# Weight sums of a seven-product block multiplication formed by accumulating transfers, with another order and other signs of the products

## The chip, the cores and the metric

The kernel runs on one core of a Trainium2 chip. Its engines are TensorE (PE, matmuls; PEld is its weight loader), VectorE (DVE), ScalarE (ACT), GpSimd (POOL) and SyncE (SP). Transfers (DMA) are issued from the queues of SP, ACT and POOL. The metric is the device time of one execution in microseconds (us). Of the kernel before, three runs were timed: median 1592.65 us, 1592.23 to 1593.92.

## The reference

One hybrid layer: normalised tokens `xn` (256 tokens, 2048 channels) and 256 context tokens `cn` are multiplied with slices of one large weight `w_in`; two branches (window attention, and a gated recurrence over 16 heads) follow, then a merge and an output projection. What matters here are two kinds of these products:

```python
aq, ak, av, ag, hq, hff, hfb, hi, hg, ma, mb = split_columns(xn @ w_in[l])
caq, cak, cav, cag, chq, chff, chfb, chi, chg, cma, cmb = split_columns(cn @ w_in[l])
g_f, k_f = hgrn_forget(hff, lb_f_all[l])
g_b, k_b = hgrn_forget(hfb, lb_b_all[l])
cg_f, ck_f = hgrn_forget(chff, lb_f_all[l])
cg_b, ck_b = hgrn_forget(chfb, lb_b_all[l])
v_h = to_heads(hi)
cv_h = to_heads(chi)
```

A forget gate is `lb + (1 - lb) * sigmoid(z)`, of which the logarithm and the rest to one are used. Keys, values (`ak`, `av`, `hi`) and the forget gates (`hff`, `hfb`) are needed of all 512 tokens.

## The kernel before, in words

Every number of the activations and of the weights is kept as a sum of two parts, high and low, and a product is high by high, low by high and high by low. ACT makes the high part of a weight chunk (`wh`, 128x1024, 512 KB), DVE the low part (`wl` = weights less `wh`); there are three buffers of each.

The stage concerned runs from about 199 us to about 660 us. It computes the columns above as 2x2 block products with seven multiplications in place of eight (a scheme of Strassen's kind). The activations' four sums are formed once (`token_sums`, L570, tile `S`). For each weight block (four quarters 11, 12, 21, 22 of 512 KB) come a set of seven products, from seven weight operands: three plain quarters and four sums of quarters. There are 23 such sets:

- `quad_tok` (L687): ten sets, from 199 to 401 us. Five outputs, each two sets long; each of the seven products has a PSUM bank of its own. A product is 24 matmuls with 256 columns.
- `quad_col` (L639): thirteen sets, from 401 to 660 us, for the forget gates. The seven products share three banks. A product is eight matmuls with 512 columns (L660) and eight with 256 (L663).

The program orders TensorE's work as it is written; the other engines' orders come from a scheduler, in which `high_priority` puts marked steps ahead. `ORDER` (L608) gives the sequence of the products within a set, and `combos` (L611) yields the weight operands in that sequence. In the kernel before, the quarters are loaded by SP (`wload`, L61, five `raw` buffers), and DVE forms the four sums by four subtractions L616 (`t` = 12-11, then 22-`t`, 12-22 in its own buffer, 21-`t`); the tile `T` for `t` alternates between two buffers; `two` (L631) then makes high and low part (ACT L635, DVE L636).

In `quad_col` a product is added onto what stands in its bank, and at fixed points a bank's content is copied or added out while the sum goes on:

```python
into = {0: (0, True), 1: (1, True), 2: (0, False), 3: (1, False), 4: (0, False), 5: (2, True), 6: (0, False)}
```

The first entry is the bank, `True` starts it afresh. After products 0 and 1 ACT copies the bank to `s15` (L667); after product 2 ACT copies bank 0 to `su` (L670); after products 3, 4 and 5 DVE adds the bank to one of these copies (`joined`, L650, its adds are L653 and L654); after product 6 ACT and DVE take half a bank each (L678, L679). The gates then go through ACT (L682, L683) and out (L685). In the order 0, 1, 2, 3, 4, 5, 6 of the kernel before, the products go to banks 0, 1, 0, 1, 0, 2, 0.

Of the kernel before, what the change touches and what calls it, by code (L numbers as in the profile page):

```python
# [38 lines left out]
def block_kernel(ctx: ExitStack, tc: tile.TileContext, x, c, cx, c_ctx, w_ada, b_ada, norm_gain, w_in,  # L39
# [521 lines left out]
    with pl("sp", reuse_waits="tile") as sp:  # L561
# [8 lines left out]
        def token_sums(g):  # L570
# [7 lines left out]

            def put(i, t):
                ks = slice(4 * g, 4 * g + 4)  # L580
                dst = [S[:, z, i, ks, :].rearrange("p k t -> p (k t)") for z in range(2)]
                act.activation(dst[0], t, AF.Copy)
                dve.tensor_tensor(dst[1], t, dst[0].bitcast(F32), op=ALU.subtract)

# [4 lines left out]
            p, q = tmp(), tmp()  # L589
            step(v(p), a21[0], a22[0], ALU.add)  # L590
            step(v(q), a21[1], a22[1], ALU.add)
            step(p, p, q, ALU.add)
            put(0, p)
            step(v(q), v(p), a11[0], ALU.subtract)
            step(v(q), v(q), a11[1], ALU.subtract)
            put(1, q)
            for i, b in ((3, a12), (2, a22)):
                step(v(p), b[0], v(q), ALU.subtract)
                step(v(p), v(p), b[1], ALU.add)
                put(i, p)  # L600
# [10 lines left out]
        def combos(b):  # L611


            def sub(o, x_, y_):
                with tc.high_priority(PRIO):
                    dve.tensor_tensor(o, x_, y_, op=ALU.subtract)  # L616
# [12 lines left out]
            yield t  # L629

# [8 lines left out]
        def quad_col(d, h0):  # L639

            co = (C_FF, C_FB)[d] + h0 * HD
            b = {n: wload(w_in, 1024 * (n[0] == "2"), 8, (co + HD * (n[1] == "2"),), HD)[0]
                 for n in ("11", "12", "22", "21")}
            m_ = [bank8() for _ in range(3)]
# [10 lines left out]

            for (i, _, mv), src in zip(ORDER, combos(b)):
                h, lo = [a.rearrange("p (k c) -> p k c", k=8) for a in two(src)]
                z, fresh = into[i]
# [6 lines left out]
                with tc.high_priority(2 * PRIO):  # L665
                    if i < 2:
                        act.activation(s15[:, i, :], m_[i], AF.Copy)  # L667
                    elif i == 2:
                        su = base.tile([P, 512], F32, tag="bb", name="su", bufs=2)
                        act.activation(su, m_[0], AF.Copy)  # L670
                    elif i == 3:
                        joined(m_[1], su, half(sg[1], 0))
                    elif i == 4:
                        joined(m_[0], s15[:, 1, :], half(sg[1], 1))
                    elif i == 5:
                        joined(m_[2], s15[:, 0, :], half(sg[0], 0))
                    else:
                        act.activation(half(sg[0], 1), pairs_of(m_[0][:, T:]), AF.Copy)  # L678
                        dve.tensor_tensor(half(sg[0], 1), pairs_of(m_[0][:, :T]), half(sg[0], 1), op=ALU.add)  # L679
            F = fp.tile([P, 2, 512], F32, tag="F0", name="F0", bufs=2)  # L680
            for i in (1, 0):
                act.activation(sg[i], sg[i], AF.Sigmoid)  # L682
                act.activation(F[:, i, :], sg[i], AF.Identity, scale=lbc[:, 2 + d, h0 + i: h0 + i + 1],  # L683
# [3 lines left out]
        def quad_tok(col0, dst):  # L687
# [5 lines left out]
            def add(o, x_, y_):  # L693
                dve.tensor_tensor(o, x_, y_, op=ALU.add)

            def done_with(i):

# [4 lines left out]
                with tc.high_priority(2 * PRIO):  # L702
                    if i < 2:
                        sn[i] = base.tile([P, 512], F32, tag="sm", name="sn", bufs=3)
                        act.activation(sn[i], m_[i], AF.Copy)
                    elif i == 2:
                        sn[2] = base.tile([P, 512], F32, tag="bb", name="sn", bufs=2)
                        add(sn[2], m_[2], sn[0])
                    elif i == 3:
                        sn[3] = base.tile([P, 512], F32, tag="bb", name="sn", bufs=2)  # L710
                        add(sn[3], sn[2], sn[1])
                        add(place(0, 1), pairs_of(m_[3]), pairs_of(sn[3]))
                    elif i == 4:
                        add(sn[2], m_[4], sn[2])
                        add(place(1, 1), pairs_of(sn[2]), pairs_of(sn[1]))
                    elif i == 5:
# [4 lines left out]
            for s in range(2):  # L721
                b = {n: wload(w_in, 1024 * (n[0] == "2") + 512 * s, 4, (col0 + T * (n[1] == "2"),), T)[0]
                     for n in ("11", "12", "22", "21")}
                for (i, _, st_), src in zip(ORDER, combos(b)):
                    h, lo = [a.rearrange("p (k c) -> p k c", k=4) for a in two(src)]
                    if s == 0:
# [838 lines left out]
```

## Time and profile before

| what | value |
|---|---|
| three timed runs | 1592.65 us median, 1592.23 to 1593.92 |
| the profiled execution's own time | 1593.52 us |
| its span, first to last instruction | 1591.7 us |
| mean granted TensorE clock | 0.998 |
| TensorE busy | 1567.9 us, 99% of the span |
| VectorE busy | 1182.9 us, 74% |
| ScalarE busy | 855.4 us, 54% |
| GpSimd busy | 140.5 us, 9% |
| `w_in` loads of 512 KB from SP | 300, median 4.5 us to landing |

How to read the profile: in the timeline each row has the start, the duration, the engine, the line, the operation, its output and inputs, how many instructions were merged, and in brackets the engine's idle time ahead and what ended it. Names are without buffer numbers, so `s` is `s15`, `pj` and `pm` are PSUM banks, `raw` is any weight buffer. Matmuls overlap, so that the durations of neighbouring rows add up to more than the time between them; the distance of two starts is the safe measure. A busy PE is not a PE at its peak.

### The profile page before, as it was taken

What the parts mean: (1) busy time and instruction counts of PE and PEld (TensorE: products, weight loads), DVE (VectorE), ACT (ScalarE), POOL (GpSimd) and SP (SyncE); (2) the same over time, 40 slices, a digit from 0 to 9 for tenths busy, and PEclk for the clock granted to TensorE, in tenths of its full rate; (3) what the DMA queues carried; (4) which work ended last, traced back from release to release, by engine and by line L of the source; (5) the groups of instructions that cost most, each with busy time, mean ns of one, the idle gap of its engine ahead of it and who ended that gap; (6) DMA issues with size and microseconds to landing.
All of it is one profiled execution on the core that took longest, in us unless ns stands there. A gap on an engine that the chain in (4) does not pass through costs nothing. (4 is left out here: it accounts for less than half of the span.)

```text
span 1591.7 us, 27553 instructions
## 1 busy us (share of the span) xinstructions
PE 1567.9 (99%) x10810; PEld 1341.4 (84%) x10810; DVE 1182.9 (74%) x1745; ACT 855.4 (54%) x1338; POOL 140.5 (9%) x280
## 2 busy tenths in 40 slices
PE   7999999999999999999999999999999999999998
PEld 4567899999888888888888888888887888888887
DVE  4449677777888887787978888887976677757764
ACT  4334443333555555655665566666565776744442
POOL 2000000000000000111121212121112000000000
PEclk9999999999999999999999999999999999999999
DMA  9995533434444444777778777787778854458761
GB/s 369 386 387 174 166 110 131 134 131 133 146 133 136 136 135 130 243 234 230 245 264 271 256 259 244 238 271 240 234 262 262 261 165 149 158 175 288 238 196 70
DMA packets 240851, 333.81 MB, mean 210 GB/s; under 512 B 12080, under 2 KB 157904, under 8 KB 239952
## 3 DMA queue, kind: packets, MB, share of 16 engines
q1 hardware_dynamic: 212048, 249.54, 48.1%
q0 software_dynamic: 19168, 64.08, 11.9%
q10 hardware_dynamic: 9504, 18.42, 3.2%
q8 instruction: 85, 1.39, 0.4%
q14 instruction: 46, 0.38, 0.1%
HBM read 300.53 MB, written 31.47 MB: 209 GB/s over the span
## 5 line engine op out<-in xcount | busy, mean ns | idle before, releaser
L85 ACT ACTIVATE wh<-raw 128x1024 fp32r<-128x1024 f32 x292 | 307.5, 1060 | 257.3 <-PE pj L101 179.1
L86 DVE TENSOR_TENSOR wl<-raw,wh 128x1024 fp32r<-128x1024 f32 x292 | 354.4, 1219 | 122.1 <-ACT wh L85 116.2
L100 PE MATMUL pj<-wh,xHL 128*128 128x512 f32 (+1 forms) x832 | 325.0, 392 | 0.7 <-ACT sg L219 0.7
L101 PE MATMUL pj<-wh,xHL 128*128 128x512 f32 (+1 forms) x832 | 320.3, 386 | 0.0
L103 PE MATMUL pj<-wl,xHL 128*128 128x512 f32 (+1 forms) x832 | 218.5, 386 | 0.0
L100 PEld LDWEIGHTS pj<-wh,xHL 128*128 128x128 f32 x832 | 156.9, 189 | 32.7 <-ACT sg L219 1.9
L101 PEld LDWEIGHTS pj<-wh,xHL 128*128 128x128 f32 x832 | 156.9, 189 | 29.9
L103 PEld LDWEIGHTS pj<-wl,xHL 128*128 128x128 f32 x832 | 154.0, 188 | 31.4
L635 ACT ACTIVATE wh<-T 128x1024 fp32r<-128x1024 f32 x69 | 73.2, 1061 | 149.6 <-DVE T L616 74.0
L635 ACT ACTIVATE wh<-raw 128x1024 fp32r<-128x1024 f32 x92 | 96.9, 1054 | 63.7 <-PE pj L734 23.4
L154 PE MATMUL pj<-xHL,wh 128*128 128x512 f32 x512 | 130.3, 395 | 0.6 <-DVE sgm L1073 0.5
L636 DVE TENSOR_TENSOR wl<-raw,wh 128x1024 fp32r<-128x1024 f32 x92 | 112.0, 1218 | 9.2 <-ACT wh L635 9.1
L154 PEld LDWEIGHTS pj<-xHL,wh 128*128 128x128 f32 x512 | 92.4, 189 | 18.0 <-DVE sgm L1073 0.9
L636 DVE TENSOR_TENSOR wl<-T,wh 128x1024 fp32r<-128x1024 f32 x69 | 84.2, 1220 | 29.7 <-ACT wh L635 29.7
L157 PEld LDWEIGHTS pj<-xHL,wl 128*128 128x128 f32 x512 | 69.9, 190 | 5.8 <-issue 0.7
L157 PE MATMUL pj<-xHL,wl 128*128 128x256 f32 x512 | 71.5, 282 | 0.6 <-issue 0.6
L204 DVE SCALAR_TENSOR_TENSOR acc<-hgw,cg,acc 128x512 f32<-128x512 f32 x60 | 44.8, 747 | 32.7 <-DMA hgw<-in_w_ada_dram 32.7
L918 DVE TENSOR_TENSOR A<-A,X 128x512 f32<-128x512 f32 x96 | 61.7, 684 | 1.6 <-ACT Kmt L848 0.7
L541 POOL DMA_DIRECT2D hgw<-in_w_ada_dram x64 | 34.8, 544 | 273.9 <-DVE acc L204 211.0
L660 PE MATMUL pm<-S,wh 128*128 128x512 f32 x224 | 56.8, 395 | 0.5 <-ACT s L667 0.5
L616 DVE TENSOR_TENSOR T<-raw,T 128x1024 f32<-128x1024 f32 x46 | 56.0, 1218 | 0.0
L616 DVE TENSOR_TENSOR raw<-raw 128x1024 f32<-128x1024 f32 x23 | 28.2, 1225 | 34.9 <-DMA raw<-in_w_in_dram 34.9
(356 smaller groups left out, 3017.9 us busy)
## 6 DMA issues: line engine op xcount, KB each, us to landing
raw<-in_w_in_dram SPq DMA_DIRECT2D x300, 512.0 KB, 4.5
raw<-in_w_ada_dram SPq DMA_DIRECT2D x64, 512.0 KB, 8.0
hgw<-in_w_ada_dram POOLq DMA_DIRECT2D x64, 256.0 KB, 4.4
raw<-in_w_o_hgrn_dram SPq DMA_DIRECT2D x32, 512.0 KB, 3.8
raw<-in_w_o_attn_dram SPq DMA_DIRECT2D x32, 512.0 KB, 4.2
raw<-in_w_out_dram SPq DMA_DIRECT2D x28, 512.0 KB, 3.6
F<-F POOLq DMA_DIRECT2D x16, 512.0 KB, 6.8
F<-F ACTq DMA_DIRECT2D x13, 512.0 KB, 4.4
```

The lines of the kernel that those rows point to most:

```text
L85: last_hi[0] = act.activation(h[:, :n], raw[:, :n], AF.Copy).ins
L86: last_lo[0] = dve.tensor_tensor(lo[:, :n], raw[:, :n], h[:, :n].bitcast(F32), op=ALU.subtract).ins
L100: pe.matmul(o, s[0], m[0], start=first, stop=False)
L101: pe.matmul(o, s[1], m[0], start=False, stop=False)
L103: pe.matmul(o, s[0], m[1], start=False, stop=last)
L154: pe.matmul(o.rearrange("p (a t) -> p a t", a=2), h[:, j, cs_], xHL[:, :, k0 + j, :T], start=k0 + j == 0, stop=False)
L157: pe.matmul(o[:, :T], lo[:, j, cs_], xH[:, k0 + j, :T], start=False, stop=k0 + j == KT - 1)
L616: dve.tensor_tensor(o, x_, y_, op=ALU.subtract)
L635: act.activation(h, src, AF.Copy)
L636: dve.tensor_tensor(lo, src, h.bitcast(F32), op=ALU.subtract)
L660: pe.matmul(m_[z].rearrange("p (z a t) -> p z a t", z=2, a=2), h[:, k, :], mv(k), start=fresh and k == 0, stop=False, skip_group_check=True)
L918: dve.tensor_tensor(av, av, f.unsqueeze(3).to_broadcast([P, 2, n2, b]), op=ALU.mult)
```

## The change

In `combos` SP fills four buffers with quarters (`u` and three `raw` buffers: 11, 21, 22, 12). GpSimd then issues three transfers per set that add a further quarter from memory onto a filled buffer (L619 of the kernel after): 22 onto the buffer with 12 (`t3`), 12 onto `u`, and, later in the set, 21 onto `u`. One sum stays with DVE (`u` + 22, L634 after). The sums have other signs, so the token sums, the combination of the products (`less`) and one sigmoid's scale change signs with them. The order of the products becomes 0, 5, 1, 3, 2, 4, 6, and in both functions the addition that followed product 3 now follows product 2. `into` is unchanged.

```diff
-        ORDER = ((0, "b11", sides(0, 0)), (1, "t1", sums(0)), (2, "t2", sums(1)), (3, "b22", sums(3)),
-                 (4, "t3", sums(2)), (5, "b21", sides(0, 1)), (6, "t4", sides(1, 1)))
+        ORDER = ((0, sides(0, 0)), (5, sides(0, 1)), (1, sums(0)), (3, sums(3)), (2, sums(1)), (4, sums(2)),
+                 (6, sides(1, 1)))
...
-            t = tmp()
-            yield b["11"]
-            sub(t, b["12"], b["11"])
-            yield t
-            sub(t, b["22"], t)
-            yield t
-            yield b["22"]
-            sub(b["12"], b["22"], b["12"])
-            yield b["12"]
-            yield b["21"]
-            sub(t, b["21"], t)
-            yield t
+            def more(t, n):
+                nc.gpsimd.dma_start(t, src(n), accum_op=ALU.add)
+
+            def raw_():
+                return wp.tile([P, 1024], F32, tag="raw", name="raw", bufs=5)
+
+            u, b21, b22, t3 = tmp(), raw_(), raw_(), raw_()
+            for t, n in ((u, "11"), (b21, "21"), (b22, "22"), (t3, "12")):
+                nc.sync.dma_start(t, src(n))
+            yield u
+            more(t3, "22")
+            more(u, "12")
+            yield b21
+            yield u
+            yield b22
+            with tc.high_priority(PRIO):
+                dve.tensor_tensor(u, u, b22, op=ALU.add)
+            yield u
+            more(u, "21")
+            yield t3
+            yield u
...
                     elif i == 2:
                         su = base.tile([P, 512], F32, tag="bb", name="su", bufs=2)
                         act.activation(su, m_[0], AF.Copy)
+                        joined(m_[1], su, half(sg[1], 0))
                     elif i == 3:
-                        joined(m_[1], su, half(sg[1], 0))
+                        pass
...
+            def less(o, x_, y_):
+                dve.scalar_tensor_tensor(o, x_, -1.0, y_, op0=ALU.mult, op1=ALU.subtract)
```

TensorE's order in the second `quad_col` set before, from its second product on (bank 0 is `pm_4105`, bank 1 is `pm_4106`, bank 2 is `pj_4107`; a row is eight matmuls, and the high part's row stands ahead of the low part's):

```order
L660 MATMUL pm_4106<-S_1263,wh_4134 128x512 x8
L663 MATMUL pm_4106<-S_1263,wl_4135 128x256 x8
L660 MATMUL pm_4105<-S_1263,wh_4156 128x512 x8
L663 MATMUL pm_4105<-S_1263,wl_4157 128x256 x8
L660 MATMUL pm_4106<-S_1263,wh_4178 128x512 x8
L663 MATMUL pm_4106<-S_1263,wl_4179 128x256 x8
L660 MATMUL pm_4105<-S_1263,wh_4201 128x512 x8
L663 MATMUL pm_4105<-S_1263,wl_4202 128x256 x8
L660 MATMUL pj_4107<-xHL_84,wh_4223 128x512 x8
L663 MATMUL pj_4107<-xHL_84,wl_4224 128x256 x8
L660 MATMUL pm_4105<-xHL_84,wh_4246 128x512 x8
L663 MATMUL pm_4105<-xHL_84,wl_4247 128x256 x8
```

No two neighbouring products go to the same bank. TensorE's order in a `quad_col` set after, likewise from its second product on (bank 0 is `pm_4614`, bank 1 is `pj_4615`, bank 2 is `pj_4616`):

```order
L672 MATMUL pj_4616<-xHL_84,wh_4651 128x512 x8
L675 MATMUL pj_4616<-xHL_84,wl_4652 128x256 x8
L672 MATMUL pj_4615<-S_1263,wh_4673 128x512 x8
L675 MATMUL pj_4615<-S_1263,wl_4674 128x256 x8
L672 MATMUL pj_4615<-S_1263,wh_4694 128x512 x8
L675 MATMUL pj_4615<-S_1263,wl_4695 128x256 x8
L672 MATMUL pm_4614<-S_1263,wh_4715 128x512 x8
L675 MATMUL pm_4614<-S_1263,wl_4716 128x256 x8
L672 MATMUL pm_4614<-S_1263,wh_4740 128x512 x8
L675 MATMUL pm_4614<-S_1263,wl_4741 128x256 x8
L672 MATMUL pm_4614<-xHL_84,wh_4762 128x512 x8
L675 MATMUL pm_4614<-xHL_84,wl_4763 128x256 x8
```

The products of banks 1, 1, 0, 0, 0 now follow each other directly: the fourth, sixth and seventh product of a set go to the bank of the one just ahead.

ScalarE's order around these places in the kernel before (the high parts `wh`, the copies L667 and L670 out of the banks, the gates L682 and L683):

```order
L667 ACTIVATE s15_4110<-pm_4105 128x512
L635 ACTIVATE wh_4201<-raw_4099 128x1024
L683 ACTIVATE F0_4091<-sg_3931,lbc_86 128x512
L667 ACTIVATE s15_4110<-pm_4106 128x512
L685 DMA F1_1_100<-F0_4091 128x1024
L635 ACTIVATE wh_4223<-raw_4103 128x1024
L670 ACTIVATE su_4176<-pm_4105 128x512
L635 ACTIVATE wh_4246<-T_4111 128x1024
```

ScalarE's order around the same copies in the kernel after (L679 and L682 are the copies; `wh_4740` is the sixth product's, `wh_4762` the seventh's from the buffer `T_4620` with the last accumulation, `wh_4804` the next set's first):

```order
L679 ACTIVATE s15_4619<-pm_4614 128x512
L696 ACTIVATE F0_4608<-sg_4441,lbc_86 128x512
L644 ACTIVATE wh_4715<-T_4620 128x1024
L698 DMA F0_3_94<-F0_4608 128x1024
L644 ACTIVATE wh_4740<-raw_4623 128x1024
L679 ACTIVATE s15_4619<-pj_4615 128x512
L644 ACTIVATE wh_4762<-T_4620 128x1024
L644 ACTIVATE wh_4804<-T_4796 128x1024
L682 ACTIVATE su_4735<-pm_4614 128x512
```

The copy to `su` now stands behind the high part of the seventh operand, which needs the transfer of 21 onto `u`, and behind the next set's first high part; the copy to `s15` of bank 1 stands behind the sixth operand's high part. On VectorE the four L616 operations of a set are gone and one add stands in their place; GpSimd's queue, which in this stage held only the stores of `quad_tok`, now holds three transfers per set.

More of the change, by code (lines that the diff above doesn't have):

```diff
@@ L577, in v, with put @@
                 return t.rearrange("p (k a t) -> p k a t", k=4, a=2)
-            def put(i, t):
+            def put(i, t, sign=1.0):
                 ks = slice(4 * g, 4 * g + 4)
                 dst = [S[:, z, i, ks, :].rearrange("p k t -> p (k t)") for z in range(2)]
-                act.activation(dst[0], t, AF.Copy)
-                dve.tensor_tensor(dst[1], t, dst[0].bitcast(F32), op=ALU.subtract)
+                act.activation(dst[0], t, AF.Copy, scale=sign)
+                if sign == 1.0:
+                    dve.tensor_tensor(dst[1], t, dst[0].bitcast(F32), op=ALU.subtract)
+                else:
+                    dve.scalar_tensor_tensor(dst[1], t, sign, dst[0].bitcast(F32), op0=ALU.mult, op1=ALU.subtract)
             def step(out, x_, y_, op):
@@ L705, in done_with @@
                         act.activation(sn[i], m_[i], AF.Copy)
+                    elif i == 3:
+                        pass
                     elif i == 2:
@@ L721, in quad_tok, with src @@
             for s in range(2):
[L722 to L725, printed above, removed]
+                def src(n):
+                    r, c0 = 1024 * (n[0] == "2") + 512 * s, col0 + T * (n[1] == "2")
+                    return w_in[r: r + 512, c0: c0 + T].rearrange("(k p) c -> p k c", p=P)
+                for (i, st_), t in zip(ORDER, combos(src)):
+                    h, lo = [a.rearrange("p (k c) -> p k c", k=4) for a in two(t)]
                     if s == 0:
```

35 lines of the change are left out of this document (16 added, 19 removed).

## The prediction

> **What bounds the kernel now.** I read the page's busy shares, then the table of stretches for the two halves of the stage, then the timeline of one `quad_col` set. The stretches (us; PE, PEld, DVE, ACT, POOL busy, clock, DMA share, GB/s):
>
> ```profile
> 200.00:400.00 200.00, 200.00 (x1669) 200.00 (x1668) 149.85 (x146) 78.12 (x81) 4.78 (x9) 1.00 0.40 129
> 400.00:660.00 260.00, 258.93 (x1475) 226.71 (x1474) 206.75 (x233) 150.34 (x194) 5.80 (x14) 1.00 0.46 139
> ```
>
> TensorE is busy without a break in both halves, at the full clock (1.00), while DVE is busy for 75 to 80% and the transfers for 40 to 46%. So time taken off DVE can only pay where TensorE waits for it. The timeline shows where TensorE's products start (`s` is `s15`):
>
> ```profile
> 420.52 2.00 PE L660 MATMUL pm<-xHL,wh 128*128 128x512 f32 x8
> 420.72 0.39 ACT L678 ACTIVATE sg<-pj 128x256 f32<-128x256 f32 x1 [1.32 <-PE pj L663]
> ...
> 423.15 1.06 ACT L635 ACTIVATE wh<-T 128x1024 fp32r<-128x1024 f32 x1 [2.05 <-DVE T L616]
> 423.31 2.00 PE L660 MATMUL pm<-S,wh 128*128 128x512 f32 x8
> 424.12 1.05 ACT L635 ACTIVATE wh<-raw 128x1024 fp32r<-128x1024 f32 x1
> ...
> 425.59 0.58 ACT L667 ACTIVATE s<-pm 128x512 f32<-128x512 f32 x1
> ...
> 426.22 2.14 PE L660 MATMUL pm<-S,wh 128*128 128x512 f32 x8
> ...
> 429.13 2.00 PE L660 MATMUL pm<-S,wh 128*128 128x512 f32 x8
> ...
> 431.17 1.06 ACT L635 ACTIVATE wh<-T 128x1024 fp32r<-128x1024 f32 x1 [1.24 <-PE pm L660]
> 431.58 1.22 DVE L636 TENSOR_TENSOR wl<-raw,wh 128x1024 fp32r<-128x1024 f32 x1
> 431.93 2.00 PE L660 MATMUL pm<-S,wh 128*128 128x512 f32 x8
> ...
> 434.72 2.00 PE L660 MATMUL pj<-xHL,wh 128*128 128x512 f32 x8
> 434.92 0.69 DVE L653 TENSOR_TENSOR s<-pm,s 128x512 f32<-128x512 f32 x1
> ...
> 440.31 2.00 PE L660 MATMUL pj<-xHL,wh 128*128 128x512 f32 x8
> ```
>
> Undisturbed products start 2.79 us apart (431.93 to 434.72; to 440.31 it is three products, 2.793 each). The one at 426.22 came 2.91 after its forerunner: it goes to bank 0, and ACT's copy L667 out of that bank ended at 425.59 + 0.58 = 426.17, 0.05 earlier. The next start too is 2.91 later, since the first row of a product that had to wait takes 2.14 instead of 2.00: a restart costs a further 0.12. A later case, with a longer wait:
>
> ```profile
> 604.17 2.11 PE L660 MATMUL pj<-S,wh 128*128 128x512 f32 x8 [0.53 <-ACT s L667]
> ...
> 607.07 1.09 PE L660 MATMUL pj<-S,wh 128*128 128x512 f32 x4
> ...
> 603.54 0.57 ACT L667 ACTIVATE s<-pj 128x512 f32<-128x512 f32 x1
> ```
>
> Copy ended 604.11, matmuls from 604.17, next start 2.90 later. This is the only kind of wait the stage has, and in sum it is small. The first matmul of `quad_tok`, then the first product of `quad_col` and the sixth of the last of 13 sets (89 starts later):
>
> ```profile
> 199.37 0.28 PE L732 MATMUL pj<-wh,xHL 128*128 128x256 f32 x1
> ...
> 400.97 2.00 PE L660 MATMUL pj<-xHL,wh 128*128 128x512 f32 x8
> ...
> 652.57 2.00 PE L660 MATMUL pj<-xHL,wh 128*128 128x512 f32 x8
> ```
>
> The latter two are 251.6 us apart; 89 x 2.793 is 248.6. All waits there together are 3.0 us. That is the most that any relief could bring in this half; the first half has none.
>
> **The change part by part.** *Fewer sums on DVE.* The groups of L616, x count, then busy us and mean ns:
>
> ```profile
> L616 DVE TENSOR_TENSOR T<-raw,T 128x1024 f32<-128x1024 f32 x46 | 56.0, 1218 | 0.0
> L616 DVE TENSOR_TENSOR T<-raw 128x1024 f32<-128x1024 f32 x23 | 28.2, 1225 | 18.7 <-DMA raw<-in_w_in_dram 18.7
> L616 DVE TENSOR_TENSOR raw<-raw 128x1024 f32<-128x1024 f32 x23 | 28.2, 1225 | 34.9 <-DMA raw<-in_w_in_dram 34.9
> ```
>
> Of these 92 operations 69 go: 69 x 1.22 = 84 us of DVE, all beside TensorE's products. On the path it is worth 0. The changed signs (`put`, `less`, the sigmoid's scale) change an operation's form, not its number or size; they too lie beside the products, within DVE's 20% of idle time: 0, and were that cover gone, a fraction of 84 us that was just freed.
>
> *Order of the products.* In a `quad_col` set the places are now: product 0 (bank 0), 5 (bank 2), 1 (bank 1), 3 (bank 1), 2 (bank 0), 4 (bank 0), 6 (bank 0). The content of bank 1 after place 3 must be copied before place 4 adds to it; bank 0 after place 5 before place 6 (copy to `su`); bank 0 after place 6 before place 7 (DVE's add L653). Before, another product lay between each time, and its 2.79 us hid the copy. Now TensorE stands still. The price from the rows: an evacuation starts 0.20 after the next product would have started (420.72 against 420.52 on ACT, 434.92 against 434.72 on DVE); a copy takes 0.58, DVE's add 0.69; the matmuls follow 0.06 later; the restart costs 0.12. On ACT the copy for place 4 is queued behind the high part for place 6, whose buffer is released 2.04 after a product's start (431.17 against 429.13), and the next ACT operation starts 0.97 after such a one (424.12 against 423.15): at 3.01, against 2.99 when the bank is ready. So ACT's copy ends at 3.59, matmuls at 3.65, which is 0.86 late, and with the restart 0.98. DVE: 0.20 + 0.69 + 0.06 + 0.12 = 1.07. In 13 sets: 26 x 0.98 + 12 x 1.07 = 38.3 us (the thirteenth wait of DVE's kind is covered, as eight matmuls of the next stage are ordered ahead of that product). The old 3.0 us go, as their two copies now have time. Net +35.3 us. `quad_tok` gives each product a bank of its own; there the new order costs nothing.
>
> The Trainium skill, "Perfetto Trace Analysis", section Matmuls, asks that independent matmul groups rotate through the PSUM banks so that one's evacuation overlaps the next one's matmuls; that speaks against this order, and the 604.17 row agrees with it.
>
> *The accumulating transfers.* The one that matters is 21 onto `u`. It is issued when the low part for place 5 is made, and the high part for place 7 reads its result; on ACT that stands ahead of the copy to `su`, for which place 6 waits. With place 3's start as zero: DVE first joins bank 2 (0.20 to 0.89), then makes the low part (1.22, to 2.11); GpSimd issues at about 2.2. Place 4 starts at 3.65, place 5 at 6.56, and ends at 9.35; the bank is ready at 9.55. ACT must by then have started two high parts, 0.97 each, the second of them not before 6.56 + 2.04 = 8.60. So a transfer that lands by 7.6, 5.4 us after its issue, costs nothing more, and each further us delays ACT's copy and TensorE by one. The trace has no accumulating transfer. The nearest is GpSimd's 512 KB load in 1 KB runs (min/median/max to landing); and SP's loads in the `quad_col` part of the stage:
>
> ```profile
> DMA to landing us min/median/max: 4.0/5.1/7.5
> ...
> q1 hardware_dynamic: 44771, 23.09, 36.1%
> ...
> raw<-in_w_in_dram SPq DMA_DIRECT2D x44, 512.0 KB, 3.9
> ```
>
> The accumulating one fetches as much and adds to what lies there. Below: as quick as the quickest plain one, 4.0. Above: twice the median, 10.2, as if the buffer were fetched by a transfer of its own. I take the middle, 7.1, as the runs are half as long (512 B) and other transfers are under way: 1.7 us late in each of 13 sets, 22.1 us. At the ends: 0, or 4.8 x 13 = 62 us. In `quad_tok` the same reckoning without waits leaves room: 70 products from 199.37 to 400.97 are 2.88 us each; four of them lie between the release of the low part's buffer and the start of the product that needs the sum, less 1.45 until the issue (0.2, then 1.22 for the low part) and 1.06 for the high part: 9.0 us, at two places in each of ten sets. At 7.1 that is 0; at 10.2 it is 20 x 1.2 = 24 us. The transfer of 22 onto `t3` starts a set ahead: 0. GpSimd's stores of `quad_tok` stand between these transfers in its queue, but wait for a set's last product only (0.20 + 0.69, so at about 1 us of the next set), before the transfers behind them are due: 0.
>
> The Trainium skill, "Collectives: The Full Stack", section The bandwidth ceiling: the fold count and why AG ≠ RS ≠ AR, holds that a reducing transfer runs at half the pace of a copy, since it reads two sources. No run here shows it yet. By it the data's share of a transfer (0.361 x 220 us / 44 = 1.8 us) counts twice, an estimate of 5.1 + 1.8 = 6.9 us, 1.5 late, and a sum 2.6 us lower than mine.
>
> *The sum.* The profiled execution took 1593.5 us, 0.9 above the median of the runs. 1593.5 + 35.3 + 22.1 = 1650.9; against the median 1650 us.
>
> **The rivals.** *Transfers hidden.* If they land within 5.4 us, only the waits for the banks remain: 1592.65 + 35.3 = 1628 us. For it: 5.1 is the median of a plain one. Against: the shorter runs and the addition. Chance 0.22.
>
> *Transfers as the bound.* If an accumulating transfer occupies the DMA engines k times as long as a plain one, a set needs 4 x 1.8 + 3k x 1.8 us of them. My set is 19.55 + 3.03 + 1.7 = 24.3 us long, so from k = 3.2 they decide. At k = 4 a set takes 28.8 instead of 19.8, 13 x 9 = 117 us, 1710 us by `quad_col` alone; if `quad_tok`'s ten sets of 20.2 us took as long, 86 us more, 1796 us. Between this and my forecast lies the case of 10.2 us, 1592.7 + 35.3 + 62 + 24 = 1714 us. For it: the DMA share is 0.46 now, and bytes grow from four quarters to seven. Against: nothing in the trace is so slow. Chance beyond 1712: 0.16.
>
> *DVE's relief quickens TensorE.* If DVE's traffic slowed the matmuls, products would become shorter without the 69 operations; the loader PEld is busy for 226.7 of 260 us only. To end faster than before, 91 products would have to win 35.3 + 22.1 us, 0.63 us each of 2.79. Against: products are 2.79 us long beside DVE's idle and busy stretches alike. It would also take no change (within 0.2%, about what a measurement of this kernel can tell from none) at a little less. Chance 0.05: faster 0.03, same 0.02.
>
> *The change not doing what it says* would be a wait left out at the three places; TensorE's rows there carry one for ACT or DVE in the order, and the sum needs the bank's content alone, so I give that no chance of its own.
>
> **How the numbers follow.** Forecast 0.57 (1635 to 1712 us), hidden 0.22, bound 0.16, relief 0.05. The point is 1650. The range leaves out the relief and the bound, 0.21 together: from 1624 (hidden, with restarts of half the price, 38 x 0.06 lower, and some slack) to 1712. Slower by over 0.2%: 0.95.
>
> **What would show it.** In the profile after: TensorE idle ahead of L672, released by ACT L679, ACT L682 and DVE L665, three times per set, some 13 x 3 rows, 0.9 us each but longer for L682; set starts about 24 us apart instead of 19.8; no gap in `quad_tok`; transfers L619 landing about 7 us after issue. It is wrong if place 6 waits no longer than place 4 (then the transfers were hidden), if `quad_tok` shows gaps (then they are slower than 9 us), or if products start 2.79 us apart throughout (then nothing of this holds).

## The result and the profile after

The kernel after took 1782.07 us (median of 4 runs, 1778.5 to 1789.1) against 1592.44 us for the kernel before (4 runs, 1591.55 to 1593.92): a ratio of 1.1195 (1.116 to 1.1231), +190 us. The direction was forecast; the size, 1650 us with a range to 1712, was not. The profiled execution of after has a span of 1779.7 us against 1591.7, +188.0.

The table of stretches, cut at the first matmul of `quad_tok`, the first of `quad_col` and the last of `quad_col`, shows where it went (length; busy us of PE, PEld, DVE, ACT, POOL; granted clock; DMA share; GB/s). First before, then after:

```profile
199.40:401.00 201.60, 201.60 (x1682) 201.60 (x1681) 150.57 (x147) 78.72 (x82) 4.78 (x9) 1.00 0.40 130
401.00:659.90 258.90, 257.83 (x1466) 225.65 (x1465) 206.63 (x232) 150.24 (x193) 5.80 (x14) 1.00 0.46 138
```

```profile
199.70:470.40 270.70, 221.23 (x1681) 217.38 (x1680) 113.75 (x114) 75.49 (x82) 43.40 (x38) 0.92 0.71 154
470.40:838.80 368.40, 291.54 (x1484) 247.38 (x1483) 169.72 (x199) 151.33 (x195) 64.27 (x53) 0.92 0.76 151
```

`quad_tok` grew by 69.1 us, for which 0 was forecast; `quad_col` by 109.5, for which 57.4 was forecast; 9.4 us lie outside. DVE is relieved as reckoned (357 to 283 us), and TensorE no longer works without a break: it stands idle, and its clock, 1.00 in both halves before, is 0.92. TensorE's waits in after, longest first (us in total, times, longest):

```profile
PE pj L672 <- ACT su L682: 30.1, 6, 5.8
PE pm L752 <- ACT wh L644: 26.2, 10, 5.6
PE pm L672 <- ACT su L682: 23.6, 6, 5.5
PE pj L752 <- ACT wh L644: 20.6, 8, 5.5
...
PE tw L955 <- DVE F L815: 5.8, 1, 5.8
```

The `su` rows are place 6 of `quad_col`, where a wait of 2.6 us (0.86 + 1.7) was forecast; it is up to 5.8. The L752 rows are `quad_tok`, where none was forecast. The last row is the head of the next stage. One `quad_tok` set on its timeline (start us, length, idle time before and what ended it):

```profile
226.88 1.27 POOL L619 DMA_DIRECT2D T<-in_w_in_dram  x1 [12.96 <-DVE wl L645]
234.74 1.06 ACT L644 ACTIVATE wh<-T 128x1024 fp32r<-128x1024 f32 x1 [8.65 <-DMA T<-in_w_in_dram]
237.09 1.23 DVE L634 TENSOR_TENSOR T<-T,raw 128x1024 f32<-128x1024 f32 x1
239.97 1.22 DVE L645 TENSOR_TENSOR wl<-T,wh 128x1024 fp32r<-128x1024 f32 x1
241.48 1.28 POOL L619 DMA_DIRECT2D T<-in_w_in_dram  x1 [5.96 <-DVE wl L645]
249.40 2.01 ACT L644 ACTIVATE wh<-T 128x1024 fp32r<-128x1024 f32 x2 [8.19 <-DMA T<-in_w_in_dram]
250.51 0.39 PE L752 MATMUL pm<-wh,xHL 128*128 128x256 f32 x1 [2.88 <-ACT wh L644]
253.74 1.28 POOL L619 DMA_DIRECT2D T<-in_w_in_dram  x1 [10.99 <-DVE wl L645]
```

Read it as a chain. Transfer 12 is issued at 226.88 and has landed at 234.64; ACT and DVE make place 3's parts, the sum with 22 and place 5's parts; 21 is issued at 241.48, 6.84 us after the landing, and lands at 249.29. Then ACT makes two high parts in a row (x2): that of place 7, and that of the **next** set's place 1. Only when the low part of the latter is made too may the next 12 be added onto that set's `u`: issue at 253.74, 4.45 us after the landing. Every us in this list is followed by the next; TensorE is not in it.

A `quad_col` set, places 3 to 7 (the copy to `su` is L682):

```profile
565.28 2.00 PE L672 MATMUL pm<-S,wh 128*128 128x512 f32 x8
567.73 1.55 POOL L619 DMA_DIRECT2D T<-in_w_in_dram  x1 [3.81 <-DVE sg L666]
568.92 2.12 PE L672 MATMUL pm<-S,wh 128*128 128x512 f32 x8 [0.69 <-ACT s L679]
571.83 2.00 PE L672 MATMUL pm<-S,wh 128*128 128x512 f32 x8
575.03 2.00 ACT L644 ACTIVATE wh<-T 128x1024 fp32r<-128x1024 f32 x2 [6.17 <-DMA T<-in_w_in_dram]
576.94 0.58 ACT L682 ACTIVATE su<-pm 128x512 f32<-128x512 f32 x1
577.57 2.83 PE L672 MATMUL pm<-S,wh 128*128 128x512 f32 x8 [2.79 <-ACT su L682]
580.20 1.91 PE L675 MATMUL pm<-S,wl 128*128 128x256 f32 x8
582.89 2.09 PE L672 MATMUL pm<-xHL,wh 128*128 128x512 f32 x8 [0.78 <-DVE s L665]
```

The three forecast waits are there (0.69, 2.79, 0.78), and 21 is issued 2.45 us after place 3's start (2.2 forecast) and lands 7.2 later. New is the product at 577.57: its eight matmuls take 2.83 us instead of 2.00. About the end of such a wait TensorE's granted clock falls to 0.5, for one or two periods of 3.41 us (here from 578.78 on).

### The profile page after: what moved, and what is told of

It is laid out like the page before. It is cut to its first block, busy times and chain, and to the rows that moved or that the text cites. A ratio compares the mean times of both kernels' runs of the same rounds, so it can differ in the third digit from the quotient of the medians.

```text
span 1779.7 us, 27665 instructions
## 1 busy us (share of the span) xinstructions
PE 1620.3 (91%) x10810; PEld 1376.9 (77%) x10810; DVE 1105.7 (62%) x1676; ACT 851.8 (48%) x1338; POOL 239.8 (13%) x349
## 3 DMA queue, kind: packets, MB, share of 16 engines
q0 software_dynamic: 75568, 100.26, 25.7%
## 5 line engine op out<-in xcount | busy, mean ns | idle before, releaser
L86 DVE TENSOR_TENSOR wl<-raw,wh 128x1024 fp32r<-128x1024 f32 x292 | 354.5, 1219 | 131.3 <-ACT wh L85 123.9
L85 ACT ACTIVATE wh<-raw 128x1024 fp32r<-128x1024 f32 x292 | 307.6, 1060 | 259.5 <-PE pj L101 175.5
L645 DVE TENSOR_TENSOR wl<-T,wh 128x1024 fp32r<-128x1024 f32 x92 | 110.9, 1221 | 297.0 <-ACT wh L644 293.1
L644 ACT ACTIVATE wh<-T 128x1024 fp32r<-128x1024 f32 x92 | 94.9, 1054 | 315.8 <-DMA T<-in_w_in_dram 258.4
L619 POOL DMA_DIRECT2D T<-in_w_in_dram x46 | 66.0, 1435 | 347.9 <-DVE wl L645 286.0
L644 ACT ACTIVATE wh<-raw 128x1024 fp32r<-128x1024 f32 x69 | 72.6, 1052 | 66.3 <-PE pj L672 32.9
L672 PE MATMUL pm<-S,wh 128*128 128x512 f32 x224 | 64.5, 435 | 30.5 <-ACT su L682 23.6
L645 DVE TENSOR_TENSOR wl<-raw,wh 128x1024 fp32r<-128x1024 f32 x69 | 84.1, 1219 | 9.5 <-ACT wh L644 9.3
L672 PE MATMUL pj<-S,wh 128*128 128x512 f32 x192 | 58.8, 456 | 34.2 <-ACT su L682 30.1
L672 PEld LDWEIGHTS pm<-S,wh 128*128 128x128 f32 x224 | 44.4, 208 | 42.1 <-ACT su L682 24.8
L672 PEld LDWEIGHTS pj<-S,wh 128*128 128x128 f32 x192 | 40.3, 221 | 44.7 <-ACT su L682 31.3
```

The costliest lines, as they stand in the source:

```text
L85: last_hi[0] = act.activation(h[:, :n], raw[:, :n], AF.Copy).ins
L86: last_lo[0] = dve.tensor_tensor(lo[:, :n], raw[:, :n], h[:, :n].bitcast(F32), op=ALU.subtract).ins
L619: nc.gpsimd.dma_start(t, src(n), accum_op=ALU.add)
L644: act.activation(h, src, AF.Copy)
L645: dve.tensor_tensor(lo, src, h.bitcast(F32), op=ALU.subtract)
L672: pe.matmul(m_[z].rearrange("p (z a t) -> p z a t", z=2, a=2), h[:, k, :], mv(k), start=fresh and k == 0, stop=False, skip_group_check=True)
```

## The experiments

After this profile, two theories. **Chain:** two landings per set and the ACT and DVE steps between them follow one another through `u`, and TensorE waits for their sum; bank waits and the halved clock matter less. **Apart:** each transfer is late (or a burden on the DMA engines) by itself, and the losses add up. For each run "+x" is its median less that of the kernel before beside it; on this scale after is at +190.

### The order alone, and with the one transfer that is not on u

`e1_order`: all sums on DVE, from the four quarters that are loaded anyway, in the new order.

```diff
-            more(t3, "22")
-            more(u, "12")
+            plus(u, t3)      # dve.tensor_tensor(u, u, t3, op=ALU.add), high priority
+            plus(t3, b22)
...
-            more(u, "21")
+            plus(u, b21)
```

> All four sums of a set are formed by DVE again, from four plain loads; signs, order and banks of the products are those of the kernel after. Theory 1 (the new order costs three bank waits per set of quad_col and nothing else, the rest of the loss belongs to the transfers): in the trace of after such a place starts 0.85 to 0.88 later and the restart costs 0.12, 3 x 0.97 on 13 sets of 19.55, less the 0.37 per set that the old order lost, is +33 us: 1626 us, range 1622 to 1635, granted clock 1.0. Theory 2 (order and signs themselves bring the long waits or the halved clock): stretches of half clock remain, and the time is above 1650 us.

Measured: 1646.5 us, +51 (ratio 1.0324, 1.0309 to 1.034), 11.5 us above the first theory's range, with no halved clock in the stage. `quad_tok` is back at 201.6 us. So theory 1's kind of loss, but more of it: place 7 waits 1.5 us instead of 0.8, since the add that it waits for is queued on DVE behind the sums, and the next stage's head waits 6.0 us as in after.

`e2_only22`: the same with `more(t3, "22")` kept.

> Of the three transfers only that of 22 onto t3 is left; DVE adds 12 and 21 onto u. Theory 1 (that transfer is ready in time, the loss hangs on the two onto u): no wait for a transfer; the three bank waits of quad_col remain, with one DVE sum less than where DVE made all four (1646 us): 1632 to 1648 us. Theory 2 (any of these transfers costs time): above 1655 us.

Measured: 1638.8 us, +44 (1.0271, 1.0255 to 1.0288). Its two stretches:

```profile
200.40:402.00 201.60, 201.60 (x1682) 201.59 (x1681) 140.62 (x135) 80.10 (x83) 17.77 (x19) 1.00 0.59 155
402.00:698.60 296.60, 269.19 (x1484) 229.87 (x1483) 196.71 (x223) 152.97 (x195) 25.30 (x28) 1.00 0.58 143
```

The order costs 37.7 us in `quad_col` and some 6 behind it; the transfer of 22 brings no wait of its own. What is left to explain, 145 us, hangs on the two transfers onto `u`.

### One transfer onto u at a time

`e3_no21` puts `plus(u, b21)` in place of `more(u, "21")`; `e4_no12` puts `plus(u, t3)` in place of `more(u, "12")`, ahead of 22's transfer.

> Of the three transfers that add, only that of quarter 21 onto u is undone: DVE adds the quarter, which is loaded anyway. Theory 1 (two transfers per set stand on one chain through u: the first lands, ACT and DVE make the parts, the second is issued, lands, ACT makes the parts of place 7 and of the next set's place 1 in this order, and only then the first of the next set is issued; in quad_tok 3.9 + 6.8 us of steps and two landings of 6.6 and 9.2 us make 26.5 us per set where TensorE needs 20.2; with one transfer left, 3.9 + 6.8 + 1.2 + 7 = 18.9 fits): no wait in quad_tok, the three bank waits in quad_col, 1626 to 1640 us. Theory 2 (each transfer is late by itself): the waits ahead of place 3 in quad_tok remain, 12 us, and similar ones may show in quad_col: above 1640 us.

> Only the transfer of 12 onto u is undone: DVE adds that quarter before 22 is added onto t3 by its transfer; 21 is still added by a transfer. Theory 1 (chain of two landings): in quad_tok one landing of 9.2 and 11.9 us of steps is 21.1 against 20.2 us, so at most 0.9 us per set, 0 to 10 us there; quad_col unchanged, as its transfer of 21 runs against place 3's start (5.4 us free, 8.7 measured): +109 us. Together 1700 to 1715 us. Theory 2 (21 is late by itself in both halves): quad_tok keeps the waits ahead of place 7, 41 us, and the slower matmuls behind them, 16 us: 1755 to 1775 us.

Measured: 1673.9 us, +79 (1.0482, 1.0459 to 1.0506), and 1684.9 us, +90 (1.056, 1.0537 to 1.0583). Their `quad_tok` stretches, without 21 and without 12:

```profile
199.30:413.90 214.60, 205.28 (x1681) 203.51 (x1680) 129.56 (x126) 77.90 (x82) 31.53 (x29) 0.99 0.70 166
```

```profile
200.10:411.90 211.80, 205.56 (x1681) 204.73 (x1680) 124.91 (x123) 77.83 (x82) 29.21 (x27) 0.98 0.73 172
```

Neither run kept to the chain theory's numbers. Without 21 the second theory's signs came: waits ahead of place 3 in `quad_tok` (9.3 us in eight of ten sets; `quad_tok` lost 13.0 us) and a time above 1640 us. 22 and 12 now leave close together and land after 9.3 us (median). The expectation's own sum had put 7 us there; with the 8.9 us that 12 takes in `quad_tok` (mean) it is 20.8 us, over TensorE's 20.2, so the wait does not contradict the chain. Without 12 the time is below both ranges. The two runs taken together speak for the chain. Over the +44 of the order, 12 alone adds 34 us and 21 alone 46; both together add 145. In `quad_tok` it is 10.2 (21 alone) and 13.0 (12 alone) against 69.1 for both.

### The price of adding

`e5_plain`: `nc.gpsimd.dma_start(t, src(n))` without `accum_op=ALU.add`.

> The three transfers overwrite instead of adding: same queue, sizes and order (the additions are left out of the computation). Theory 1 (the addition makes the transfer long: 6.6 and 8.7 to 9.2 us to landing where plain loads of the trace before took 5.1): landing falls to 5 to 5.5 us, the chain in quad_tok to 10.7 + 10.5 = 21 us (+0 to 10 us), quad_col keeps the bank waits (+33 us): 1625 to 1650 us. Theory 2 (GpSimd's queue and the traffic of seven quarters make them late, not the addition): landing stays at 6.5 to 9 us, and the time within 15 us of 1782 us.

The sums then lack the three added quarters; only the time says something.

Measured: 1655.3 us, +60 (1.0376, 1.0353 to 1.04), 5 us above the first theory's range. Landing of the three, without the addition and then in after (min, median, max), and GpSimd's queue (packets, MB, share):

```profile
DMA to landing us min/median/max: 3.8/5.0/7.1
...
q0 software_dynamic: 29104, 100.26, 18.9%
```

```profile
DMA to landing us min/median/max: 5.7/7.5/11.0
...
q0 software_dynamic: 75568, 100.26, 25.7%
```

The same bytes go in 2.6 times the packets of the whole queue, of which 19168 packets stand in the kernel before as well: per transfer it is (75568 - 19168) / 69 = 817 packets adding and (29104 - 19168) / 69 = 144 plain. In engine time: the queue holds the DMA engines for 0.257 x 1779.7 = 457 us in after, 0.189 x 1654.6 = 313 without the addition, and 0.119 x 1591.7 = 189 before, when the 69 transfers did not exist; so one of them takes (313 - 189) / 69 = 1.8 us plain and 3.9 adding. This also tests the chain. Averaged over the ten sets of `quad_tok`, in order (12 from issue to landing, steps, 21 from issue to landing, steps): 7.25 + 6.75 + 9.15 + 4.15 = 27.3 us in after, 4.75 + 6.92 + 5.54 + 4.15 = 21.4 without the addition. The sets are 27.1 and 21.0 us long. What the landings lost, 6.1 us, was taken off the set, which is then within 0.8 us of TensorE's own 20.2.

### The third transfer's share

`e8_no22` puts `plus(t3, b22)` in place of `more(t3, "22")`.

> Only the transfer of 22 onto t3 is undone (DVE adds it); 12 and 21 onto u stay transfers. This transfer was reckoned to cost nothing, as t3 is needed late. Theory 1 (it costs by lengthening the others, which share GpSimd's queue with it: with a neighbour 8.7 to 10.9 us to landing, without 5.7 to 6.9): landing falls to 6 to 7 us, quad_tok's chain to 10.7 + 1 + 12.7 = 24.4 us, +4 per set instead of 6.9, quad_col's wait at place 6 to about 2 us: 1690 to 1720 us. Theory 2 (the others are long by themselves): within 12 us of 1782 us.

Measured: 1772.5 us, +176 (1.1103, 1.1083 to 1.1123). The first theory missed, and the time is in the second's range: 21 lands after 8.05 and 7.94 us (mean of `quad_tok`, `quad_col`) instead of 9.15 and 8.72, not after 6 to 7, and DVE's extra sum of 1.2 us lengthens a step (7.8 instead of 6.75 in `quad_tok`). In this kernel the neighbour costs 21 about 1 us.

### The halved clock

`e6_warm`: TensorE is kept busy while it waits for place 6; what it computes goes into a spare bank and is not used.

```diff
+                if i == 4:
+                    for k in range(16):
+                        pe.matmul(spare..., S[:, 0, 0, k % 8, :P], mv(k % 8), start=k == 0, stop=k == 15)
```

> The kernel after, with 16 matmuls of 512 columns (16 x 0.25 = 4.0 us) into a spare bank that nobody reads, ahead of the product at place 6 of each quad_col set, where TensorE stands 2.6 to 5.8 us. Theory 1 (TensorE's clock is halved because it stood still for some us): the half clock on place 6, 45 us of it in the 13 sets, goes, and 22 us with it; where the wait is under 4.0 us (about 4 sets) the extra matmuls cost about 1 us each: 1757 to 1766 us. quad_tok, which is not touched, keeps its half clock on place 7. Theory 2 (the half clock has another cause, as the load on the DMA engines): the rows of place 6 stay as slow, and the time is 1782 us or a little above.

Measured: 1769.1 us, +173 (1.1086, 1.1059 to 1.1114): 17 us of the 190 by the two ratios, with a few us of uncertainty, and 3 us above the first theory's range. The stretches:

```profile
198.90:465.40 266.50, 218.69 (x1681) 214.60 (x1680) 113.79 (x114) 75.50 (x82) 43.44 (x38) 0.94 0.71 156
465.40:826.10 360.70, 322.51 (x1692) 271.86 (x1691) 169.22 (x199) 149.97 (x195) 64.31 (x53) 0.98 0.78 154
```

That the standing still is the cause is confirmed: in `quad_col`, where TensorE was kept busy, the clock rises from 0.92 to 0.98, and on place 6 the half clock falls from 45.3 to 9.8 us; in `quad_tok`, which was not touched, it stays low. But place 6 became 1.2 us shorter and the wait ahead of it 0.55 longer: about half of the gain was handed back to the chain, and `quad_col` shrank by 7.7 us, not by 15.5.

The Trainium skill, "TensorE: Matmul & The Clock Gate", Part 1, says that the array falls to half clock after an idle window of about 3.4 us, and that the window runs freely. The halving agrees, as does the length of 3.41 us; the trace is stricter on the wait. In after no wait below 2.0 us was followed by half clock, of ten from 2.0 to 3.0 us six were, and in the stage all fifteen from 3.9 us on, the nine from 4.47 us on for 6.83 us.

Which of the ten, the trace tells as well. The half-clock stretches of after start on a fixed grid: 223.79, 251.10, 274.99 and 305.71 us are 8, 7 and 9 times 3.413 us apart. The wait from 247.63 to 250.51 us lies almost whole (2.82 us) in one such period, that from 247.69 to 251.10, and half clock follows. The longer wait from 600.85 to 603.81 is split at 602.67 into 1.82 and 1.14 us, and the clock stays. Over the whole stage of after, each full-clock period in which TensorE stood for 2.06 us or more was followed by half clock, and none in which it stood for 1.82 us or less. In the other versions the shortest such time that was followed by half clock is 1.72 us and the longest that was not is 1.87. So it takes somewhat more than half a period of standing, not a whole one, and whether a wait of 2 to 3 us costs the clock depends on where it falls.

### Lengthening and opening the chain

`e12_longer` adds two operations to the chain, `dve.tensor_scalar(u, u, 1.0, None, op0=ALU.mult)`, ahead of `more(u, "21")`.

> The kernel after with two more DVE operations on u (times 1.0, in place) ahead of the transfer of 21 in each of the 23 sets; the sums are unchanged. Theory 1 (chain): TensorE stands idle for some 5 us per set and DVE for more, yet each set grows by the two operations' whole length: 23 x 2 x their mean, 1.1 to 1.2 us by the other operations of this size, +50 to +57 us: 1825 to 1845 us. Theory 2 (the transfers' pace or TensorE with its clock sets the length; DVE has slack): within 12 us of 1782 us.

Measured: 1818.0 us, +223 (1.1397, 1.1375 to 1.142).

```profile
L638 DVE TENSOR_SCALAR T<-T 128x1024 f32<-128x1024 f32 x46 | 31.8, 691 | 0.8
```

```profile
200.20:481.90 281.70, 226.48 (x1682) 222.54 (x1681) 130.67 (x136) 76.17 (x82) 44.13 (x39) 0.91 0.68 149
481.90:876.00 394.10, 304.64 (x1468) 255.49 (x1467) 186.44 (x223) 154.45 (x195) 63.32 (x51) 0.90 0.71 141
```

The operations are shorter than I assumed, 0.69 us: 31.8 us of work on an engine with slack cost 34 us. That excludes the second theory, but that the two numbers nearly agree is partly luck. `quad_tok` grew by 11 us and `quad_col` by 26. In `quad_tok` the steps between 12's landing and 21's issue became 3.5 us longer, not 1.4, as other low parts now come in between on DVE (so in the set from 223 to 253 us); and 21, issued later, misses its neighbour and lands after 6.3 us instead of 9.15. What does show the chain is that its four terms again add up to the set: 7.87 + 10.26 + 6.31 + 3.91 = 28.4 us, where a set takes 28.2; in `quad_col` 30.2 and 30.3.

`e9_apart` adds 12 onto a second copy of 11.

```diff
-            u, b21, b22, t3 = tmp(), raw_(), raw_(), raw_()
+            u, v, b21, b22, t3 = raw_(), tmp(), raw_(), raw_(), raw_()
...
-            more(u, "12")
+            more(v, "12")    # v holds 11 as well; v takes u's place behind place 1
```

> 12 is added onto a second copy of 11, which SP loads for it (a fourth raw tile per set), so that it need not wait until the parts of place 1 are made; all three transfers stay, and the traffic of a set grows from seven quarters to eight. Theory 1 (chain of two landings): 12 leaves the chain; in quad_tok one landing of 9.2 us and some 11 us of steps fit into 20.2: 0 to 15 us lost there instead of 69; quad_col as before, its 21 runs against place 3's start: 1710 to 1735 us. Theory 2 (traffic, or each transfer late by itself): landings grow, and the time is 1770 us or more.

Measured: 1798.5 us, +202 (1.1266, 1.1244 to 1.1289). By the number this is the second theory's case, and the landings grew to 8.4 us (median of all three transfers). `quad_tok` fell to 237.6 us, 36 above before where 0 to 15 were expected, and no product there waits at place 3 any more, but `quad_col` rose to 417.3: with four raw tiles per set in five buffers `t3` is loaded late, 22's transfer waits for it on GpSimd, and 21 stands behind it in the queue. A second change came with the first, so this run decides nothing for `quad_col`.

`e7_order2` exchanges products 2 and 3, so that two of the three bank waits vanish; the sum with 22 and the transfer of 21 move one product ahead with it.

```diff
-... (1, sums(0)), (3, sums(3)), (2, sums(1)), (4, sums(2)), ...
+... (1, sums(0)), (2, sums(1)), (3, sums(3)), (4, sums(2)), ...
```

> All three transfers stay; the order is 0, 5, 1, 2, 3, 4, 6 (products 2 and 3 exchanged), so that in quad_col only place 7 follows a product in its own bank, and 21 is issued one product earlier. Theory 1 (chain of two landings through u and the bank waits): the bank waits of places 4 and 6 go, 13 x 1.9 = 25 us; the steps between the landing of 12 and the issue of 21 shrink by one low part, 1.2 us, in quad_tok, and a product's 2.8 us in quad_col: 12 and some 30 us: 1705 to 1735 us. Theory 2 (only the bank waits shrink, the transfers are late whenever they are issued): 1750 to 1762 us.

Measured: 1758.8 us, +162 (1.1028, 1.0997 to 1.1059). The stretches:

```profile
199.60:454.20 254.60, 217.27 (x1682) 213.10 (x1681) 113.48 (x113) 75.50 (x82) 42.30 (x38) 0.95 0.74 163
454.20:821.80 367.60, 290.02 (x1482) 248.00 (x1481) 167.99 (x200) 148.82 (x194) 65.26 (x53) 0.91 0.77 153
```

A miss, and a telling one. The time lies in the second theory's range, but by luck: that theory let `quad_col` shrink by its bank waits, and there `quad_col` takes 367.6 us instead of 368.4, although place 4 no longer waits and the content of `su` is complete a product earlier. What came back, 16 us, came back in `quad_tok`, mostly because 21 lands there after 7.47 us instead of 9.15. In `quad_col` the time went into the wait for `su`, whose copy stands behind place 7's high part on ACT (63.6 us against 53.7). The chain's four terms are now 6.82 + 7.13 + 9.00 + 4.54 = 27.5 us of a set of 28.3 (367.6 / 13). In after they would be 6.61 + 6.75 + 8.72 + 3.93 = 26.0 without waiting for TensorE, an estimate with the 6.75 us that the first steps take in `quad_tok`; so there TensorE's own path of 28.3 us a set came last. What TensorE gains, the chain takes.

`e10_ahead` keeps everything, and makes the next set's first parts ahead of place 7's. On ACT the two high parts (the x2 above) change places; 12 of the next set is then issued before 21 has landed. DVE's two low parts change places with them, and the next set's loads stand earlier in the program too.

```diff
+                if n + 1 < len(srcs):
+                    g = combos(srcs[n + 1])
+                    first, second = two(next(g)), next(g)
+                yield two(next(g_))      # place 7
```

> The kernel after with the same transfers, order and banks, but the parts of the next set's place 1 are made ahead of those of place 7, so that ACT and DVE have them done, and GpSimd issues 12 of the next set, while 21 is still under way. Theory 1 (the set's length is that of the chain 12 lands, 6.8 to 8.4 us of steps, 21 lands, 4 us of steps, next 12): the chain is open, TensorE's own pace rules again; in quad_tok at most about 10 us are left as where 12 was undone (21 has 8 us there and takes up to 9), quad_col keeps the bank waits and the late 21 of about 2 to 4 us a set: 1680 to 1715 us. Theory 2 (the DMA engines or GpSimd's queue cannot bring three such transfers in less than 27 us): 1765 to 1800 us.

Measured: 1706.2 us, +112 (1.0689, 1.067 to 1.0708). 78 us came back from the order in which two operands are split. One pair of transfers in `quad_tok`, 21 and then 12 of the next set, which leaves 3.4 us before 21 lands (at 325.43):

```profile
316.78 1.28 POOL L619 DMA_DIRECT2D T<-in_w_in_dram  x1 [2.73 <-DVE wl L645]
322.01 1.28 POOL L619 DMA_DIRECT2D T<-in_w_in_dram  x1 [3.95 <-DVE wl L645]
```

`quad_tok`, then `quad_col`:

```profile
199.00:413.80 214.80, 204.85 (x1681) 203.43 (x1680) 116.89 (x114) 78.95 (x82) 43.91 (x39) 0.99 0.88 194
413.80:769.20 355.40, 287.05 (x1484) 244.00 (x1483) 171.25 (x199) 153.52 (x195) 63.82 (x52) 0.93 0.77 155
```

`quad_tok` lost 55.9 of its 69.1 us with all three transfers in place, at a DMA share of 0.88: their pace was not the limit. Over the +44 of the order both transfers now add 67 us; by themselves they added 34 and 46. `quad_col` gave back 13 us only: there 21 is late against TensorE's own path as well.

`e11_ahead2` does both: open chain and exchanged products.

> As the kernel with the next set's first parts ahead, and with the order 0, 5, 1, 2, 3, 4, 6 besides. Theory 1 (with the chain open, bank waits count again, and so does the earlier issue of 21): two bank waits of 0.95 us go in 13 sets, 25 us, and 21 starts up to 2.8 us earlier; the copy su still stands behind the high part of place 7 on ACT: 20 to 50 us below the kernel with the old order, 1640 to 1685 us. Theory 2 (the pace of the transfers rules in both): within 10 us of each other.

Measured: 1655.8 us, +61 (1.0374, 1.0358 to 1.0389), 50 below the run before it.

```profile
199.40:420.30 220.90, 207.83 (x1682) 206.21 (x1681) 118.91 (x116) 79.65 (x83) 44.52 (x39) 0.98 0.86 192
420.30:714.50 294.20, 269.58 (x1482) 234.69 (x1481) 167.46 (x196) 151.54 (x194) 63.38 (x51) 0.97 0.94 187
```

In `quad_col` the exchange of the products is worth 61 us with the chain open (355.4 to 294.2) and 1 us with it closed (368.4 to 367.6); `quad_tok` is 6 us longer than in the run before. (The profiled execution of that run lay 6 us above its median, so the 61 may be a few us too many.) That is what a chain of nearly equal length beside TensorE's path does: each hides what the other would gain. No version here beats the kernel before; the nearest, +44, keeps one transfer of three.

## Why the prediction was wrong

**The bank waits** were right in mechanism and size: 35.3 us forecast, 37.7 measured where they stand alone (296.6 against 258.9). Not foreseen were the 5.8 us at the next stage's head, which come with the order too (6.0 where DVE makes all sums; before shows no such wait), with 6.83 us of half clock about their end: together most of the 9.4 us outside the two halves. Why DVE makes the tile `F` late there was not tried.

**22 onto t3** was put at 0, and it brings no wait of its own; it lengthens 21's landing by about 1 us.

**21 in `quad_col`** (22.1 us forecast) was right in mechanism, wrong in size. The reckoning holds where the landing is what I took: in the set shown it is 7.20, the transfer is there 9.65 us after place 3's start, 2.05 past the 7.6 that cost nothing, and place 6 is 0.86 + 2.05 = 2.91 late by the reckoning, 2.95 by the rows (577.57 - 571.83 - 2.79). The term that was mis-sized is the landing: 8.72 us in the mean, not 7.1. By the starts of the products, place 6 comes 48 us later in the 13 sets than where the order stands alone. The plain landing that the estimate started from, 5.1 us of four loads, was right (5.0 for 69 here). The Trainium skill's half pace ("Collectives: The Full Stack"), cited in the prediction and stated there for the reduce step of a ring of ranks, is near the engine time of one transfer, 1.8 and 3.9 us; the time to landing, on which the sum rested, the estimate by it (6.9 us) puts too low.

**The clock** is missing in the sum. The forecast waits were held to cost their length plus 0.12 us of restart; waits of over 2 us mostly halve the clock behind them as well, for 45 us on place 6. By the starts, place 7 follows place 6 by 5.51 us instead of 3.98, 20 us in 13 sets. Bank waits 37.7, late landing 48 and clock 20 make 106 of the 109.5 us in `quad_col`. This says where TensorE lost the time; it is not what each would give back by itself, as the chain there is nearly as long.

**The step that failed** is this one: "In `quad_tok` the same reckoning without waits leaves room: ... 9.0 us, at two places in each of ten sets. At 7.1 that is 0". Both places were measured against TensorE's unhindered pace, each as if the other transfer were on time. The first error is small: alone, 21 has some 6.7 us, not 9.0 (where 12 was undone, landings of 7.8 to 8.7 us brought waits of 1.0 to 2.3, and 21 left 3.7 to 4.1 us after place 3's start in these sets, where 1.45 were reckoned). The second is the large one: the slack of one transfer is the other's. 12 may be issued only when the next set's place 1 is split, and ACT and DVE do that behind place 7's split, which waits for 21 (ScalarE's order shown ahead of the prediction has it: `wh_4804`, the next set's first, stands right behind `wh_4762`); 21 may be issued only when place 5 is split, which waits for 12. Around this loop a set of 20.2 us has 20.2 - 6.75 - 4.15 = 9.3 us for **both** landings; they take 16.4. The difference, 7.1 us, is what a set grew by (6.9), and opening the loop gave 55.9 of 69.1 us back. The sign that the prediction named, gaps in `quad_tok`, came, but not for the reason beside it: 12 landed after 7.25 us in the mean, well under 9, and place 3 waited for it 10 us in all.

**The rivals.** Transfers as the bound came nearest in time, but not as the mechanism: k is 3.9 / 1.8 = 2.2, under the 3.2 from which they were to decide, and with the chain open `quad_col` runs in 22.6 us a set (294.2 / 13) with the same transfers. At its DMA share of 0.94 they may be next; that was not tried. That transfers are hidden is refuted by the waits, and that DVE's relief quickens TensorE by its products: where nothing hinders them, they still start 2.88 and 2.79 us apart.

## What to carry to other kernels

When a step moves from an engine in order to a transfer, follow its operand once around the loop: what must be done before the transfer may start, what is queued on the in-order engines behind the one who waits for it, and whether that is the next round's trigger. Slack is to be shared by all transfers on such a loop, and when a wait behind TensorE is removed, ask for the loop's length before counting the gain. Look at the trace for a set length that equals landings plus steps; exchanging two operations on an engine can then be worth more than any of the waits.

## What the runs showed of the hardware

- A 512 KB transfer that adds (512 B and 1 KB runs, DRAM onto a filled tile) took 7.5 us to land (median) against 5.0 for the same one that overwrites, 3.9 against 1.8 us of all 16 DMA engines, and 817 packets against 144; GpSimd's issue of it took 1.28 us in `quad_tok` and 1.55 in `quad_col`, against 0.75 and 0.88 where it overwrites.
- Where two such transfers left together (22 and 12, with 21 undone), they landed after 9.3 us (median). Where none of the others was under way, they took 6.4 us (median; 22 as the only transfer) and 7.8 (12 and 21, with 22 undone).
- TensorE's granted clock falls to 0.5 for one or two periods of 3.41 us when it stood still for 2.06 us or more of a full-clock period; it did not fall at 1.82 us or less (both in after). At the same load on the DMA engines (share 0.76 and 0.78), matmuls that nobody reads, put into the wait, cut the half clock on that product from 45.3 to 9.8 us.
